# Every third output store of a tree-attention kernel gives its last sixteen rows to two small hardware DMAs

## The chip, the cores and the metric

The kernel runs on one core of one Trainium2 chip. The metric is the device time of one execution in microseconds (us), the median of three runs. A profile of one execution shows the engines of the core: TensorE (PE, with its weight loads as PEld), VectorE (DVE), ScalarE (ACT), GpSimd (POOL) and SyncE (SP), and beside them 16 DMA engines, which move data between HBM and SBUF for all of them. "Rows" below are SBUF partitions, of which there are 128.

## The reference

For 8 batches and 12 heads, 96 heads in all, each of 512 queries of 64 elements attends only to itself and its ancestors in a binary tree (the parent of node `i` is `(i - 1) // 2`):

```python
scores = np.einsum('bhqd,bhkd->bhqk', Q, K) * scale
scores = scores + (1 - mask) * (-1e9)
weights = np.exp(scores - np.max(scores, axis=-1, keepdims=True))
weights = weights / (np.sum(weights, axis=-1, keepdims=True) + 1e-10)
return np.einsum('bhqk,bhkd->bhqd', weights, V).astype(np.float32)
```

Q, K, V and the output are float32, 12.58 MB each.

## The kernel before, in words

Row `p` of a tile holds nodes `4p` to `4p + 3` of a head, so one head is 1 KB (256 float32) on each of the 128 rows, and that KB lies in one piece in HBM. Heads are worked on in pairs (48 of them, `NP`); two pairs make a quad of four heads (24, `NQ`), which is one output tile `of` and one store; two quads make a group of eight heads (12, `NO`), which is the unit of loading.

The main loop (line 498) makes one pass for each pair `i`: scores on TensorE (lines 310 to 351), their exponential on ScalarE (lines 323 and 347), the products with V for the pair before (`values`, line 366), the division by the sums on VectorE (`norm`, lines 392 and 395, which writes `of`), and the transposes of Q and K for a pair further on (line 275), which VectorE copies out of PSUM (line 301). V is spread into the order that the products need by copies on VectorE (lines 238 and 253), ScalarE (line 253) and GpSimd (line 224).

All loads but the first small ones, and 23 of the 24 stores, are DMAs that GpSimd issues[...]; the stores share that queue. `pool_program` (line 412) writes out their order by hand: for each group half of K, half of Q, all of V, the other half of K, then the four copies of line 224, the other half of Q, and then two stores, eight quads behind the loads' own count (`BEHIND`, line 409). Stores 0 to 13 go between the loads, stores 14 to 22 after them. A store is 512 KB: on each row four pieces of 1 KB. The output tiles have 15 buffers (line 158), so a quad can wait long for its store.

SyncE has almost nothing to do: it issues the first K load and two small loads of mask codes (8 rows and 40 rows, lines 175 and 176) at the start, and two of the three pieces of the last store at the end (lines 522 and 523; ScalarE issues the third). Between them its queue is idle.

Of the kernel before, what the change touches and what calls it, by code (L numbers as in the profile page):

```python
# [115 lines left out]
def kernel(  # L116
# [7 lines left out]
    nc = tc.nc  # L124
    B, H, S, D = Q.shape
    P = nc.NUM_PARTITIONS
# [3 lines left out]
    NP = 2 * NQ  # L130
# [9 lines left out]
    Or = out.rearrange("b h (p t) d -> p (b h) (t d)", t=4)  # L140
# [61 lines left out]
    qTs, kTs, kqps, obs, ets, ofs = {}, {}, {}, {}, {}, {}  # L202
# [10 lines left out]
    def load_k(o, h0=0, n=8):  # L213
        load(ksts, "kst", loads, Kr, o, h0, n)

    def load_q(o, h0=0, n=8):
        load(qsts, "qst", loads, Qr, o, h0, n)

    def load_v(o, h0=0, n=8):
        load(vsts, "vst", vloads, Vr, o, h0, n)  # L220

    def spread_top(eng, o, h0=0, h1=8):
        for j in range(4):
            eng.tensor_copy(  # L224
                out=vts[o % NV][32 * j:32 * j + 32, h0:h1, VTOP:VTOP + D],
                in_=vsts[o][0:32, h0:h1, UNITS[TOP + j][1], :],
            )
# [21 lines left out]
    def spread_l7(copy, o, quad, h0=0, h1=8):  # L249

        slot = 2 * (quad % 2)
        lower = quad < 2
        copy(  # L253
            out=tile_pair(o, 0, h0, h1, 1)[32 * quad:32 * quad + 32] if lower
            else tile_pair(o, 64, h0, h1, 0)[32 * quad - 64:32 * quad - 32],
            in_=swapped(vsts[o][32:64, h0:h1, slot + (not lower), :], D if lower else -D),
        )
# [21 lines left out]
    def transpose(i):  # L279
        kqp = psT.tile([P, 2, 1024], bf16, name="kqp")  # L280
        kqps[i] = kqp
        for t in range(4):
            for a in range(2):
                transpose_one(kqp[:, 0, :], i, a, t, _slot_layout(t)[1], ksts, perms[t])
        for t in range(4):
            for a in range(2):
                transpose_one(
                    kqp[:, 1, :], i, a, t, [_psum_unit(4 * QPOS[t] + j) for j in range(4)],
                    qsts, qperm,
                )  # L290
# [17 lines left out]
    def scores1(i):  # L308

        sp = psS.tile([P, 2, 512], fp32, name="s1")  # L310
        for a in range(2):
            nc.tensor.matmul(  # L312
                out=sp[:, a, :], lhsT=k1code[64 * a:64 * a + 64, :],
                rhs=q1code[64 * a:64 * a + 64, :], start=True, stop=False,
            )
        for a in range(2):
            nc.tensor.matmul(  # L317
                out=sp[:, a, :], lhsT=keys(i, a, TOP),
                rhs=qTs[i][64 * a:64 * a + 64, :, :].rearrange("p t c -> p (t c)"),
                start=False, stop=True,  # L320
            )
        et = etpool.tile([P, 2, 4, 128], bf16, name="e1")
        nc.scalar.activation(  # L323
            out=et[:, :, :, :].rearrange("p a t c -> p (a t c)"),
            in_=sp[:, :, :].rearrange("p a c -> p (a c)"),
            func=AF.Exp, scale=scale,
        )
        ets[i] = et

    def scores2(i):  # L330

        sp = psS.tile([P, 2, 4, 128], fp32, name="s2")
        for a in range(2):
            nc.tensor.matmul(  # L334
                out=sp[:, a, :, 32:128], lhsT=k2code[64 * a:64 * a + 64, :],
                rhs=q2code[64 * a:64 * a + 64, :].rearrange("p (t c) -> p t c", t=4),
                start=True, stop=False,
            )
        for tile2, lo, hi in ((2, 32, 192), (0, 192, 320), (1, 320, 384), (3, 416, 512)):
            for a in range(2):  # L340
                nc.tensor.matmul(  # L341
                    out=sp[:, a, :, :].rearrange("p t c -> p (t c)")[:, lo:hi],
                    lhsT=keys(i, a, TILE2[tile2]),
                    rhs=qTs[i][64 * a:64 * a + 64, :, :].rearrange("p t c -> p (t c)")[:, lo:hi],
                    start=False, stop=tile2 == 3, skip_group_check=tile2 in (2, 0),
                )
        nc.scalar.activation(  # L347
            out=e2s[i % NE][:, :, :, 32:128].rearrange("p a t c -> p (a t) c"),
            in_=sp[:, :, :, 32:128].rearrange("p a t c -> p (a t) c"),
            func=AF.Exp, scale=scale,  # L350
        )
# [31 lines left out]
    def norm(i):  # L383
        q, r = divmod(i, 2)
        if r == 0:
            ofs[q] = opool.tile([P, 4, 4, D], fp32, name="of")
        ob = obs[i][:, :, 0:261]
        part, bank = list(ob.ap[0]), list(ob.ap[1])
        sums = bass.AP(ob.tensor, ob.offset, [part, bank, [195, 2], [65, 2]])
        vals = obs[i][:, :, 1:261].rearrange("p a (t c) -> p a t c", c=D + 1)[:, :, :, 0:D]  # L390
        rec = small.tile([P, 2, 4, 1], fp32, name="rec")
        nc.vector.reciprocal(  # L392
            out=rec[:, :, :, :].rearrange("p a (x y) z -> p a x (y z)", x=2), in_=sums
        )
        nc.vector.tensor_tensor(  # L395
            out=ofs[q][:, 2 * r:2 * r + 2, :, :],
            in0=vals,
            in1=rec[:, :, :, :].to_broadcast([P, 2, 4, D]),
            op=ALU.mult,
        )  # L400

    def store(eng, q, h0=0, n=4):
        eng.dma_start(  # L403
            out=Or[:, 4 * q + h0:4 * q + h0 + n, :],
            in_=ofs[q][:, h0:h0 + n, :, :].rearrange("p h t d -> p h (t d)"),
        )


    BEHIND = 8
    NO = NQ // 2  # L410

    def pool_program():

        load_k(0, 2, 2)
        load_q(0, 2, 2)
        load_v(0, 0, 4)
        load_k(0, 4, 4)
        load_q(0, 4, 4)
        load_v(0, 4, 4)
        load_k(1, 0, 4)  # L420
        load_q(1, 0, 4)
        spread_top(nc.gpsimd, 0, 0, 4)
        load_v(1)
        load_k(1, 4, 4)
        load_q(1, 4, 4)
        spread_top(nc.gpsimd, 0, 4, 8)
        yield
        yield
        for o in range(2, NO):
            load_k(o, 0, 4)  # L430
            load_q(o, 0, 4)
            load_v(o)
            load_k(o, 4, 4)
            spread_top(nc.gpsimd, o - 1)
            load_q(o, 4, 4)
            yield
            for q in (2 * o - BEHIND, 2 * o + 1 - BEHIND):
                if q >= 0:
                    store(nc.gpsimd, q)
        for q in range(NQ - BEHIND, NQ - 1):  # L440
            yield
            store(nc.gpsimd, q)
            if q == NQ - BEHIND + 1:
                spread_top(nc.gpsimd, NO - 1)

    def spread_first(copy, quad, parts):

        for part in parts:
            if part < 4:
                spread_l7(copy, 0, part, 4 * quad, 4 * quad + 4)  # L450
            else:
                spread_leaves(0, part - 4, 4 * quad, 4 * quad + 4)

    def spread_vector(i):
# [4 lines left out]
        o, step = divmod(i + (2 if i > 4 else 1), 4)  # L459
        if 1 <= o < NO and step < 2:  # L460
            if i <= 4:
# [9 lines left out]
    def spread_scalar(i):  # L471

        if i == 1:
            spread_first(nc.scalar.copy, 1, (0, 1))
        o, quad = divmod(i + 1, 4)
        if 2 <= o < NO and quad < 2:
            spread_l7(nc.scalar.copy, o, quad)
        if i == 4:
            for quad in (0, 1):
                spread_l7(nc.scalar.copy, 1, quad)  # L480

    def pool_until(done, wanted):
        while done < wanted:
            next(program, None)
            done += 1
        return done
# [11 lines left out]
    for i in range(NP + 1):  # L498
        if i < NP:
            scores1(i)  # L500
            scores2(i)
            spread_scalar(i)
        if i == 1:
            transpose(2)
            evac(2)
            spread_first(nc.vector.tensor_copy, 1, (2, 3))
        if i >= 1:
            values(i - 1)
            norm(i - 1)
        for n in (1 if i == 0 else i + 2,):  # L510
            if n < NP:
                transpose(n)
                evac(n)
        if i == 0:
            spread_first(nc.vector.tensor_copy, 0, range(6))
        spread_vector(i)
        if steps < NO:
            steps = pool_until(steps, min((i + 11) // 4, NO))
        else:
            steps = pool_until(steps, min(steps + 2, NO + (i - 2) // 2 - (NQ - 1 - BEHIND)))  # L520
        if i == NP - 1:
            store(nc.sync, NQ - 1, 0, 2)
# [32 lines left out]
```

## Time and profile before

Three runs took 137.17, 137.59 and 138.16 us. The profiled execution has a span of 135.9 us from the first to the last instruction.

| engine | busy us | share of the span | instructions |
|---|---|---|---|
| TensorE | 109.6 | 81% | 2409 |
| VectorE | 105.0 | 77% | 220 |
| ScalarE | 106.8 | 79% | 123 |
| GpSimd | 96.0 | 71% | 140 |

Busy time is the sum of the instructions' durations; what counts more is what an engine waits for, and when. The profile also has a row for the DMA engines, with their mean busy share in 40 slices of the span, and a list of DMA queues: the GpSimd queue carries 30.68 MB, SyncE's queue 0.71 MB, ScalarE's 0.46 MB, and TensorE's instructions come in 19 transfers of 16 KB. A store that GpSimd issues takes 10.4 us (median) from issue to landing, the two pieces that SyncE issues at the end 5.4 and 4.7 us.

### The profile page before, as it was taken

The page shows a single profiled execution, that of the slowest core. Times are in us where ns is not written, and L with a number is a line of the kernel's source. Part 1 is how long each engine was busy: PE and PEld are TensorE (multiplying, and loading weights), DVE is VectorE, ACT ScalarE, POOL GpSimd, SP SyncE. Part 2 cuts the span into 40 slices and gives each one's busy share as a digit, 9 for nine tenths or more (in the row PEclk, how much of TensorE's full clock was granted, in tenths as well). Part 3 has the DMA queues.
Part 4 walks back from the last instruction along what each step waited for, and adds up shares of the span by engine and source line. Part 5 has one row for each costly group of instructions (what it writes and reads, how often), then busy time and mean ns, then how long its engine had stood idle before and what let it go on. Part 6 is the DMA issues. An engine that isn't in the chain of part 4 may idle for free.

```text
span 135.9 us, 5534 instructions
## 1 busy us (share of the span) xinstructions
PE 109.6 (81%) x2409; PEld 78.7 (58%) x2409; DVE 105.0 (77%) x220; ACT 106.8 (79%) x123; POOL 96.0 (71%) x140
## 2 busy tenths in 40 slices
PE   4977885996997989998979979879959679878700
PEld 1354664774775766766757657667737457647500
DVE  6559988798898897797897797997697697797510
ACT  4166789699699799897899799897897888897600
POOL 6987979398697984983974697597597597393200
PEclk9999999999999999999999999999999999999995
DMA  3999999999999999999999999999999999999980
GB/s 102 233 174 196 198 196 198 196 197 197 197 197 237 321 197 221 333 200 203 345 201 200 336 218 197 317 239 198 294 262 197 269 292 195 250 392 375 379 305 25
DMA packets 41978, 32.19 MB, mean 237 GB/s; under 512 B 1458, under 2 KB 39010, under 8 KB 41954
## 3 DMA queue, kind: packets, MB, share of 16 engines
q0 software_dynamic: 40640, 30.68, 124.7%
q1 hardware_dynamic: 754, 0.71, 1.6%
q10 hardware_dynamic: 560, 0.46, 1.0%
q8 instruction: 19, 0.31, 0.8%
q14 instruction: 5, 0.04, 0.1%
HBM read 37.87 MB, written 12.58 MB: 371 GB/s over the span
## 4 chain that ended last, share of the span: by engine, by line
DVE 37%; PE 36%; DMA 9%; ACT 7%; issue 5%; ACTq 0%; DVEq 0%
PE ob L366 14%; DVE of L395 11%; DVE vt L253 10%; DMA vst<-in_V_dram 9%; PE kqp L275 7%; DVE kq L301 7%; DVE vt L238 6%; PE s L312 5%; ACT e L323 4%; DVE rec L392 3%; PE s L317 3%; PE ob L263 3%; PE s L341 3%; ACT e L347 2%; PE s L334 2%
## 5 line engine op out<-in xcount | busy, mean ns | idle before, releaser
L323 ACT ACTIVATE e<-s 128x1024 bf16<-128x1024 f32 x48 | 49.0, 1020 | 16.2 <-PE s L317 15.7
L366 PE MATMUL ob<-vt,e 128*128 128x65 bf16 (+1 forms) x940 | 37.9, 197 | 10.5 <-DVE of L395 8.2
L366 PEld LDWEIGHTS <-e 128*128 128x128 bf16 (+1 forms) x960 | 30.6, 102 | 17.3 <-PE s L341 6.1
L224 POOL COPY vt<-vst 32x512 bf16<-32x512 bf16 (+1 forms) x52 | 31.5, 605 | 10.4 <-DMA vst<-in_V_dram 5.7
L347 ACT ACTIVATE e<-s 128x768 bf16<-128x768 f32 x48 | 38.4, 801 | 0.0
L301 DVE COPY kq<-kqp 128x1024 bf16<-128x1024 bf16 x48 | 32.7, 681 | 2.5 <-PE kqp L275 2.4
L395 DVE TENSOR_TENSOR of<-ob,rec 128x512 f32<-128x512 f32 x47 | 32.5, 691 | 1.6
L208 POOL DMA_DIRECT2D kst<-in_K_dram x24 | 18.5, 771 | 11.6 <-DMA vst<-in_V_dram 10.5
L253 ACT COPY vt<-vst 32x1024 bf16<-32x1024 bf16 (+1 forms) x24 | 24.1, 1002 | 1.7 <-DMA vst<-in_V_dram 1.0
L275 PE MATMUL kqp<-ptile,qst 128*64 128x128 bf16 x384 | 19.1, 220 | 2.5 <-DMA qst<-in_Q_dram 2.5
L275 PE MATMUL kqp<-ptile,kst 128*64 128x128 bf16 x384 | 19.5, 220 | 1.9 <-issue 1.8
L403 POOL DMA_DIRECT2D out_dram<-of x23 | 17.4, 762 | 3.7 <-DVE of L395 3.5
L208 POOL DMA_DIRECT2D qst<-in_Q_dram x24 | 18.4, 768 | 2.1 <-PE s L317 0.6
L392 DVE RECIPROCAL rec<-ob 128x8 f32<-128x8 f32 x47 | 9.7, 206 | 13.2 <-PE ob L366 12.6
L312 PE MATMUL s<-codes 64*128 64x512 bf16 x96 | 19.1, 386 | 0.8 <-issue 0.2
L341 PEld LDWEIGHTS <-kq 64*128 64x128 bf16 x384 | 15.8, 94 | 6.2 <-issue 0.7
L317 PE MATMUL s<-kq 64*128 64x512 bf16 x96 | 18.5, 376 | 0.7 <-DVE kq L301 0.7
L341 PE MATMUL s<-kq 64*128 64x128 bf16 (+3 forms) x384 | 17.7, 209 | 0.4 <-issue 0.4
L253 DVE COPY vt<-vst 32x1024 bf16<-32x1024 bf16 (+1 forms) x28 | 16.8, 600 | 0.6
L334 PE MATMUL s<-codes 64*128 64x384 bf16 x96 | 15.9, 323 | 0.4
L238 DVE COPY vt<-vst 64x1024 bf16<-64x1024 bf16 (+1 forms) x26 | 13.0, 499 | 3.7 <-DMA vst<-in_V_dram 1.9
L275 PEld LDWEIGHTS <-qst 128*64 128x64 bf16 x384 | 13.5, 110 | 3.3 <-DMA qst<-in_Q_dram 3.1
(24 smaller groups left out, 54.1 us busy)
## 6 DMA issues: line engine op xcount, KB each, us to landing
out_dram<-of POOLq DMA_DIRECT2D x23, 512.0 KB, 10.4
kst<-in_K_dram POOLq DMA_DIRECT2D x23, 256.0 KB, 11.6
qst<-in_Q_dram POOLq DMA_DIRECT2D x23, 256.0 KB, 9.6
vst<-in_V_dram POOLq DMA_DIRECT2D x11, 512.0 KB, 12.6
vst<-in_V_dram POOLq DMA_DIRECT2D x2, 256.0 KB, 6.1
first_k<-in_K_dram SPq DMA_DIRECT2D x1, 256.0 KB, 3.3
first_q<-in_Q_dram ACTq DMA_DIRECT2D x1, 256.0 KB, 3.6
out_dram<-of SPq DMA_DIRECT2D x1, 256.0 KB, 5.4
```

Of the source, the lines that this page charges most:

```text
L208: nc.gpsimd.dma_start(out=kept[o][:, h0:h0 + n, :, :].rearrange("p h t d -> p h (t d)"), in_=src[:, 8 * o + h0:8 * o + h0 + n, :],)
L224: eng.tensor_copy(out=vts[o % NV][32 * j:32 * j + 32, h0:h1, VTOP:VTOP + D], in_=vsts[o][0:32, h0:h1, UNITS[TOP + j][1], :],)
L253: copy(out=tile_pair(o, 0, h0, h1, 1)[32 * quad:32 * quad + 32] if lower else tile_pair(o, 64, h0, h1, 0)[32 * quad - 64:32 * quad - 32], ...
L275: nc.tensor.transpose(out=dst, in_=st[i // 4][:, 2 * (i % 4) + a, t, :], identity=perm)
L301: nc.vector.tensor_copy(out=kq[:, :, :, :].rearrange("p k (x y) c -> p k x (y c)", x=2), in_=src)
L312: nc.tensor.matmul(out=sp[:, a, :], lhsT=k1code[64 * a:64 * a + 64, :], rhs=q1code[64 * a:64 * a + 64, :], start=True, stop=False,)
L317: nc.tensor.matmul(out=sp[:, a, :], lhsT=keys(i, a, TOP), rhs=qTs[i][64 * a:64 * a + 64, :, :].rearrange("p t c -> p (t c)"), start=False, ...
L323: nc.scalar.activation(out=et[:, :, :, :].rearrange("p a t c -> p (a t c)"), in_=sp[:, :, :].rearrange("p a c -> p (a c)"), func=AF.Exp, s ...
L341: nc.tensor.matmul(out=sp[:, a, :, :].rearrange("p t c -> p (t c)")[:, lo:hi], lhsT=keys(i, a, TILE2[tile2]), rhs=qTs[i][64 * a:64 * a + 6 ...
L347: nc.scalar.activation(out=e2s[i % NE][:, :, :, 32:128].rearrange("p a t c -> p (a t) c"), in_=sp[:, :, :, 32:128].rearrange("p a t c -> p ...
L366: nc.tensor.matmul(out=ob[lo:hi, a, start_o:start_o + 65], lhsT=e[:, a, QPOS[t], lo:hi], rhs=vt[:, 2 * (i % 4) + a, col:col + 65], **flags,)
L395: nc.vector.tensor_tensor(out=ofs[q][:, 2 * r:2 * r + 2, :, :], in0=vals, in1=rec[:, :, :, :].to_broadcast([P, 2, 4, D]), op=ALU.mult,)
```

## The change

For the quads with `q % 3 == 1` (1, 4, 7, 10, 13, 16, 19 and 22, eight of them) GpSimd's store covers rows 0 to 111 only. Rows 112 to 119 and 120 to 127 go out in two DMAs of their own, of 32 KB each, which SyncE issues as soon as the quad's second `norm` is done. So these sixteen rows leave in time order of the computation, some eight quads before GpSimd's part of the same store. The work of the engines, the order of the loads and the output stay as they were. It is meant to shift a part of the output from GpSimd's queue to SyncE's idle one, and from all 16 DMA engines to those that an 8-row DMA runs on.

```diff
-    def store(eng, q, h0=0, n=4):
+    def store(eng, q, h0=0, n=4, rows=(0, 128)):
+        p = slice(*rows)
         eng.dma_start(
-            out=Or[:, 4 * q + h0:4 * q + h0 + n, :],
-            in_=ofs[q][:, h0:h0 + n, :, :].rearrange("p h t d -> p h (t d)"),
+            out=Or[p, 4 * q + h0:4 * q + h0 + n, :],
+            in_=ofs[q][p, h0:h0 + n, :, :].rearrange("p h t d -> p h (t d)"),
         )
+    def parted(q):
+        return q % 3 == 1
+    def store_main(q):
+        store(nc.gpsimd, q, rows=(0, PARTED if parted(q) else P))
+    def store_rest(q):
+        if parted(q):
+            for p in range(PARTED, P, 8):
+                store(nc.sync, q, rows=(p, p + 8))
     BEHIND = 8
+    PARTED = 112
...
-                    store(nc.gpsimd, q)
+                    store_main(q)
         for q in range(NQ - BEHIND, NQ - 1):
             yield
-            store(nc.gpsimd, q)
+            store_main(q)
...
             values(i - 1)
             norm(i - 1)
+            if i % 2 == 0 and i < NP:
+                store_rest(i // 2 - 1)
```

## The prediction

> **What bounds the kernel now.** I read the slices of the span first, then the stages, the queues, the waits near the end and the chain that ended last. In the slices the DMA row is full nearly throughout, and no other row is:
>
> ```profile
> DVE  6559988798898897797897797997697697797510
> ACT  4166789699699799897899799897897888897600
> DMA  3999999999999999999999999999999999999980
> ```
>
> In the table of stages (columns: stage, its us, busy us of PE, PEld, DVE, ACT, POOL with counts, clock, DMA share, GB/s) the DMA engines are over 1, since packets of one engine overlap, until 130 us:
>
> ```profile
> 98.00:117.60 19.60, 16.20 (x388) 12.11 (x389) 15.38 (x29) 16.66 (x20) 13.87 (x20) 1.00 1.36 244
> 117.60:126.00 8.40, 6.71 (x140) 4.64 (x139) 7.21 (x15) 7.25 (x9) 5.72 (x8) 1.00 1.07 370
> 126.00:130.00 4.00, 2.31 (x52) 1.65 (x49) 2.23 (x5) 1.92 (x3) 0.76 (x1) 1.00 1.00 374
> 130.00:135.90 5.90, 0.00 (x0) 0.00 (x0) 0.00 (x0) 0.00 (x0) 0.00 (x0) 0.66 0.37 131
> ```
>
> The last 5.9 us hold nothing but stores. The packets in the trace say what one row costs: GpSimd's loads come as 512 B packets that start 41.2 ns apart on one engine, its stores as one 4 KB packet a row, one each 164 ns. An engine has 36352 / 16 = 2272 load packets and 2944 / 16 = 184 store packets: 93.6 + 30.2 = 124 us of a span of 136. So DMA is the bound, with the computation close behind. The waits from 100 us on show where the two meet (engine, line, releaser: us, times, longest), and the chain has one V load in it:
>
> ```profile
> DVE vt L238 <- DMA vst<-in_V_dram: 1.9, 2, 1.0
> PE kqp L275 <- DMA qst<-in_Q_dram: 0.6, 1, 0.6
> ```
>
> ```profile
> 104.92 12.62 DMA vst<-in_V_dram
> ...
> 128.99 0.69 DVE of L395
> ```
>
> VectorE stops 1.0 us each for the last two V loads and TensorE 0.6 for the last Q load; after V at 117.5 us come 12 us of computation, then the last stores.
>
> **The 16 engines are not level.** A transfer is complete when its slowest engine is, and the trace has the 16 moments at which each completion counter rises. For the last V load they lie, after the first, at 0, 0.12, 0.13, 0.39, 0.98, 1.24, 1.42, 1.77, and 2.10, 2.27, 2.33, 2.35, 2.58, 2.63, 2.98, 3.18 us: the load waits 3.2 us for its last engine. The queues name the cause:
>
> ```profile
> q0 software_dynamic: 40640, 30.68, 124.7%
> q8 instruction: 19, 0.31, 0.8%
> ```
>
> 0.8% of 16 x 135.9 us over 19 transfers is 0.92 us for each 16 KB of instructions, during which one engine moves nothing else. After eight of them (67 us) eight engines are some 1.07 us further back than at 15 us, after sixteen (117 us) the same eight about 2.1; the other eight gained none. So the instruction transfers go round eight of the sixteen, and these eight are the late ones. At the end the pattern is the same: at 125.5 us the late eight stand at 2.12 to 4.58, the early eight at 0 to 1.79.
>
> [...]the 8-row load of mask codes raised its counter in 8 steps after one early one, the 40-row load in 10.[...]
>
> **The change part by part.** Per parted store:
> - removed: on every engine one row of GpSimd's store, 0.164 us;
> - added: on engines 0 to 7 two rows of four 1 KB packets. The hardware stores and first loads of this kernel show 46 ns a packet, starting 42 apart: 2 x 4 x 46 = 0.37 us, 0.33 at the least.[...] I take 0.37[...].
> - so engines 8 to 15 have 0.164 us less, engines 0 to 7 0.20 us more. Eight times: -1.31 and +1.64 us.
> - issue: SyncE needs 0.39 us a DMA (lines 522 and 523). Its queue waits for the second `norm` of the quad, but all that it has behind that is the next such pair and, after the last, the final store:
>
> ```profile
> SPq L403 <- DVE of L395: 127.3, 2, 126.5
> ```
>
>  So the wait delays no one. GpSimd's DMA instructions (0.76 us) stay as many; 15 output buffers hold. I cost these at nothing.
>
> **Which half is the late one** decides the sign. No view names the engines. The trace gives a clue: the 40-row load[...]. Six of its ten ends lie at 4.21 to 4.39 us, and three, at 4.307, 4.334 and 4.363, are each followed on their engine by 16 packets and an end of GpSimd's first load (4.970, 4.997, 5.027). Followed on through ends at 6.987, 7.014, 7.043 to 8.327, 8.351, 8.381, they are third to fifth of the five leading engines, none of which ever takes an instruction transfer.[...] Stalls at 6.5 to 7.5 us make the middle step unsure. I take it: the change unloads the late half.
>
> At the end the late half's last engine then goes from 4.58 to about 4.58 - 7 x 0.164 = 3.43 at 125.5 us, the early half's from 1.79 to 1.79 + 7 x 0.20 = 3.2: still behind, but little. The end comes up to 1.3 us earlier. Against that, by the last V load SyncE has sent seven pairs (2.6 us on engines 0 to 7) while only five shortened stores (-0.8) have passed: early half 1.77 + 1.76 = 3.5, late half 3.18 - 0.82 = 2.4. V lands 0.3 us later, and with it the computation; the last stores, which today trail `norm` (129.7) by 4.9 us behind backlog, absorb that. The sum: -1.3 + 0.3 = -1.0, 136.6 us.
>
> **Rivals.**
> - The late half is 0 to 7. Then V and Q land 1.7 us later, the stalls in the waits grow, and the end has +1.6: 139.2, slower. For it: nothing but the weak step above. 15%.
> - Hidden: the 0.3 us at V, or a second engine of the early half that becomes last, eats the gain: 137.5. For it: both halves come within 0.3 us of each other. 27%.
> - [...]engines 0 to 7 carry 8 us more, of which some 3 were slack: 142. 6%.
> - Waits for V and Q (2.5 us together) shrink too, and all of it reaches the end: 135.6. For it: at the V load before, 3.18 falls to about 2.8. 12%.
> - The forecast, 136.6: 40%.
>
> **How the numbers follow.** Faster by over 1% is below 136.2: the case of 135.6 and the lower third of the forecast's spread (0.5 us either way), 0.12 + 0.2 with a little of the rest, 0.35. Slower than 139.0: [...], 0.17. Between: 0.48. The range[...]: 135.7 to 139.2.
>
> **What would show it.** Right: 16 DMAs of 32 KB on SyncE's queue landing in a few us; at 117 us completion spread over both halves, with the last V load within 0.5 us of 117.5; the stores-only stretch at the end about 1 us shorter. Wrong: packets of SyncE's queue well over 46 ns[...]; V and Q landing over 1 us later with longer stalls on lines 238 and 275 (wrong half); or an unchanged tail.

## The result, and the profile after

The changed kernel takes 141.28 us (median of four runs, 140.83 to 141.62), the kernel before 137.78 us beside it (137.17 to 138.16). The ratio is 1.0256, with a 95% interval of 1.0206 to 1.0307: 3.5 us slower. Measured again later (e17 below), the same change came to 1.0211 (1.0150 to 1.0273); that run gives a second profile of it. The forecast was 136.6 us with a range up to 139.2, so both the side and the size were missed. Executions over 1.5% above the fastest of their kernel are left out of every ratio here as slow (one of e3 took 318.6 us), which also lowers the ratio of a kernel that scatters widely of itself: with every execution counted, e9 below has 1.0108 instead of 1.0082, and e6 1.0158 instead of 1.0114.

The span grew from 135.9 to 139.1 us. The slices of the changed kernel, VectorE, ScalarE and DMA, and below them the bytes that the DMA engines moved:

```profile
DVE  6459989698878897768797697997897697697500
ACT  4156789599679799888899698998896897897500
DMA  3999999999999999999999999999999999989970
GB/s 96 228 172 193 195 196 198 203 197 196 199 199 255 289 199 244 316 198 221 323 203 222 316 203 223 322 212 216 309 220 209 310 219 204 335 332 309 309 247 24
```

The DMA row is as full as before and no other row filled up. In the stages (same columns as the table of before, cut at the same work: up to the last V load, to some 3.7 us ahead of the end of the last `norm`, to that end, and the rest):

```profile
100.50:120.10 19.60, 16.15 (x382) 11.91 (x379) 14.98 (x28) 16.75 (x19) 13.37 (x19) 1.00 1.37 239
120.10:128.50 8.40, 6.26 (x138) 4.43 (x134) 7.23 (x15) 6.98 (x9) 5.69 (x8) 1.00 0.96 330
128.50:132.15 3.65, 2.29 (x52) 1.65 (x49) 2.20 (x5) 1.90 (x3) 0.72 (x1) 1.00 0.94 310
132.15:139.10 6.95, 0.00 (x0) 0.00 (x0) 0.00 (x1) 0.00 (x0) 0.00 (x0) 0.56 0.42 134
```

After the last V load the DMA engines are nearly as busy as before (0.96 and 0.94 against 1.07 and 1.00), but they move 330 and 310 GB/s where they moved 370 and 374. Each byte became dearer, and nearly all of that is after the last V load: up to it the rate is 239 GB/s against 244. The stretch after the last `norm`, forecast to be 1 us shorter, is 6.9 us instead of 6.2. The other part lies ahead of it. First the issues of the V loads, before and after (the number after "to" is the moment of the last issue), then two lines of the changed kernel's chain:

```profile
L208 POOL DMA_DIRECT2D vst<-in_V_dram x13: 777/884/927, 2.8 to 104.9; - x13
```

```profile
L208 POOL DMA_DIRECT2D vst<-in_V_dram x13: 760/884/929, 2.8 to 107.1; - x13
```

```profile
96.43 12.80 DMA vst<-in_V_dram
...
131.46 0.69 DVE of L395
```

The last `norm` ends at 132.15 us and not at 129.68, since the last V load was complete at 120.02 us and not at 117.54. That load took hardly longer (12.9 us against 12.6); it was issued 2.2 us later. The V load before it, the first line of the chain here, was already complete 2.2 us later than before (109.22 us against 107.02), so most of the delay had gathered over the groups before. In this profile 2.5 of the 3.2 us come from there and 0.7 from the end. In the second profile the shares are 1.8 and 1.9 us, with the same sum within 0.5: where the time shows is not fixed, so the experiments below look at the total.

The parts that the prediction took for granted are there. The queues of the changed kernel, its DMA issues, and what SyncE's queue waits for:

```profile
q0 software_dynamic: 40512, 30.15, 121.8%
q1 hardware_dynamic: 1394, 1.23, 2.9%
q8 instruction: 19, 0.31, 0.8%
```

```profile
out_dram<-of POOLq DMA_DIRECT2D x8, 448.0 KB, 10.5
out_dram<-of SPq DMA_DIRECT2D x16, 32.0 KB
```

```profile
SPq L404 <- DVE of L395: 121.8, 8, 20.2
```

Eight stores of 448 KB, sixteen DMAs of 32 KB, half a megabyte moved from GpSimd's queue (30.68 MB before) to SyncE's, and eight waits of SyncE for `norm` with nothing but its own pieces behind them. Before the last of them, the last packet of a pair moved 4.3 to 5.2 us after the pair's first issue, where GpSimd's stores need 10.5 us to land, so SyncE's packets did not wait behind GpSimd's. Each small DMA raises its completion counter in 8 steps after one early one, and GpSimd's stores of 112 rows raise theirs in 16, as those of 128 do: they run on eight engines and on sixteen. "Engines 0 to 7", in the prediction and below, stands for the eight that carry an 8-row DMA; which ones they are is not shown.

The packets tell the two rates apart (worked out from the packet records: GpSimd's store packets of 4 KB, one row each, and the small ones of 1 KB):

```
kernel    4 KB packets between loads    after 124 us: number, mean ns, over 230 ns    1 KB packets between loads
before    162 to 163 ns                 608, 174.2, 10                                -
after     162 to 163 ns                 685, 202.2, 115                               384, 55.6 ns
```

In the changed kernel a figure takes GpSimd's stores of 112 and of 128 rows together. Between the loads the shorter stores leave the mean where it was (162.8 ns against 162.5). At the end, where nothing but stores is left, they don't.

### The profile page after: what moved, and what is told of

Same layout as the page of the kernel before. It is cut to its first block, busy times and chain, and to the rows that moved or that the text cites. A ratio compares the mean times of both kernels' runs of the same rounds, so it can differ in the third digit from the quotient of the medians.

```text
span 139.1 us, 5562 instructions
## 1 busy us (share of the span) xinstructions
PE 109.9 (79%) x2409; PEld 79.3 (57%) x2409; DVE 105.4 (76%) x220; ACT 107.1 (77%) x123; POOL 95.5 (69%) x140
## 4 chain that ended last, share of the span: by engine, by line
PE 29%; DVE 28%; DMA 26%; issue 7%; ACT 3%; POOL 1%; DVEq 0%; ACTq 0%; POOLq 0%
PE ob L366 11%; DMA vst<-in_V_dram 9%; DMA kst<-in_K_dram 9%; DMA qst<-in_Q_dram 8%; DVE vt L253 8%; DVE of L395 8%; PE kqp L275 6%; DVE kq L301 5%; DVE vt L238 5%; PE s L312 3%; PE ob L263 3%; PE s L317 2%; DVE rec L392 2%; PE s L341 2%; ACT e L347 2%
## 5 line engine op out<-in xcount | busy, mean ns | idle before, releaser
L238 DVE COPY vt<-vst 64x1024 bf16<-64x1024 bf16 (+1 forms) x26 | 13.5, 521 | 3.5 <-DMA vst<-in_V_dram 1.6
L275 PEld LDWEIGHTS <-kst 128*64 128x64 bf16 x384 | 12.9, 111 | 4.9 <-issue 3.7
## 6 DMA issues: line engine op xcount, KB each, us to landing
out_dram<-of POOLq DMA_DIRECT2D x15, 512.0 KB, 10.5
out_dram<-of POOLq DMA_DIRECT2D x8, 448.0 KB, 10.5
```

Of the source, the lines that this page charges most:

```text
L275: nc.tensor.transpose(out=dst, in_=st[i // 4][:, 2 * (i % 4) + a, t, :], identity=perm)
```

## The experiments

Each is set against the kernel before on the same chip. "Parted" quads are those whose store is divided. Quads 1, 4, 7, 10 and 13 are stored by GpSimd between the loads (early), 16, 19 and 22 after the last V load (late). Times in us are the ratio less 1, times 137.7. A moment read from a single profile is sure to about 1 us only: three kernels that do the same work up to the last V load (before, and the two below with only late stores altered and no small DMAs) had it at 117.54, 117.69 and 118.55 us.

| kernel | late store of GpSimd | small DMAs | ratio (95%) | us | after 124 us: ns a packet | last `norm` to end, us |
|---|---|---|---|---|---|---|
| before | 128 rows | none | 1 | 0 | 174 | 6.2 |
| the change | 112 | early, late | 1.0256 (1.0206 to 1.0307) | +3.5 | 202 | 6.9 |
| early quads only (e1) | 128 | early | 1.0032 (1.0012 to 1.0053) | +0.4 | 176 | 6.5 |
| late quads only (e2) | 112 | late | 1.0225 (1.0173 to 1.0277) | +3.1 | 200 | 8.5 |
| late shape alone (e9) | 112 | none | 1.0082 (1.0057 to 1.0106) | +1.1 | 201 | 5.8 |
| late small ones alone (e11) | 128 | late, extra | 1.0044 (1.0019 to 1.0070) | +0.6 | 173 | 5.7 |
| early small ones alone (e12) | 128 | early, extra | 1.0095 (1.0061 to 1.0130) | +1.3 | 171 | 5.1 |
| late in two of 64 rows (e6) | 64 and 64 | none | 1.0114 (1.0077 to 1.0150) | +1.6 | 201 | 8.3 |
| late by whole head (e5) | 128 | one of 128 KB each | 1.0051 (1.0027 to 1.0075) | +0.7 | 176 | 5.4 |

### Early against late

One theory was that the late stores lose the time through their shape; the rival, that the five early pairs push back the V loads.

```diff
-        return q % 3 == 1
+        return q % 3 == 1 and q < 14      # e1: early quads only
+        return q % 3 == 1 and q >= 14     # e2: late quads only
```

> Only the five parted stores that leave between the loads (quads 1, 4, 7, 10, 13); the three in the store-only stretch at the end are whole again. Theory HALF (the small DMAs load engines 0 to 7, one of which is the last to complete V; a pair costs them 8 x 53 ns less 164 ns, net 0.26 us): the last V load lands 5 x 0.26 = 1.3 us later than before, time about 139.1. Theory TAIL (stores of 112 rows slow each other where all engines store): the 4 KB packets from 124 us on fall back to about 175 ns, and the time is close to before, 137.8 to 138.3. Theory EARLY (the sixteen rows overtake loads, whatever engines they run on): like HALF, 5/7 of it.

> Only the parted stores of quads 16, 19 and 22; the five between the loads are whole. HALF: by the last V load two pairs have gone and no store is shorter, so engines 0 to 7 are 2 x 0.42 = 0.85 us later; the last V load about 0.8 us later, time 138.5 or less. TAIL: the 4 KB packets of the store-only stretch take over 200 ns as in the changed kernel, and most of its loss is here: 139.5 to 141.

The early five cost 0.4 us, the late three 3.1, both in the range of theory TAIL, and the two make up the whole (3.5). Five eighths of the change explain an eighth of the loss.

### Parts of the change, all eight quads

```diff
-            if i % 2 == 0 and i < NP:
-                store_rest(i // 2 - 1)         # e3: no small DMAs
...
-            for p in range(PARTED, P, 8):
-                store(nc.sync, q, rows=(p, p + 8))
+            store(nc.sync, q, rows=(PARTED, P))   # e4: one of 16 rows
```

e3 leaves rows 112 to 127 of the eight quads unwritten.

> All eight stores of 112 rows stay and the small DMAs are left out, so rows 112 to 127 of eight quads are not written. HALF and EARLY: every engine has 5 x 0.164 = 0.8 us less before the last V load and 1.3 us less in all, so 136.3 to 137. TAIL: the packets of the store-only stretch stay at over 200 ns although no small DMA runs, and the time stays above before's, 138 to 139.5.

> The sixteen rows leave in one DMA of 16 rows[...], at the same moments on the same queue. HALF: no engine gets more than 4 x 53 - 164 = 0.05 us a quad, the last V load at 117.5 to 118.2, so the loss but for the tail's goes: 138 to 139. EARLY: as slow as the changed kernel, 141. TAIL: the 4 KB packets of the store-only stretch stay over 200 ns.

e3: 1.0064 (1.0030 to 1.0098), 0.9 us slower than before, though every engine has 8 x 0.164 = 1.3 us less to move. Its packets after 124 us take 194 ns. So shorter stores lose time with nothing added. e4: 1.0157 (1.0112 to 1.0203), above the 138 to 139 us of theory HALF. Sixteen rows in one DMA instead of two, meant for sixteen engines instead of eight, win back 1.4 us (0.4 to 2.3, by the two intervals); 2.2 us stay, with packets of 206 ns at the end. The engines are then complete 2.9 us apart at the last V load, those of the change 5.3. So the imbalance that the prediction turned on is, by these figures, less than half of the loss.

### The shape of a late store

Three ways to alter only GpSimd's stores of quads 16, 19 and 22. e5 parts by heads: GpSimd stores three heads and SyncE the fourth, both on 128 rows. e6 has GpSimd store rows 0 to 63 and 64 to 127 in two DMAs. e9 stores 112 rows and leaves rows 112 to 127 of these three quads unwritten.

```diff
+        return q % 3 == 1 and q >= 14
...
-        store(nc.gpsimd, q, rows=(0, PARTED if parted(q) else P))
+        store(nc.gpsimd, q, n=3 if parted(q) else 4)                     # e5, and store(nc.sync, q, 3, 1)
+        for rows in ((0, 64), (64, 128)) if parted(q) else ((0, 128),):  # e6, no small DMAs
+            store(nc.gpsimd, q, rows=rows)
```

> In quads 16, 19 and 22 SyncE takes the fourth head of the quad on all 128 rows (128 KB, one DMA on 16 engines) instead of sixteen rows; GpSimd stores three heads on 128 rows. As many bytes leave early as in the run with parted stores after the last V load, and twice over. TAIL (the shape of 112 rows is what hurts): a GpSimd packet is 3 KB here and takes 125 to 140 ns, none over 200 ns as a rule; 137.0 to 138.2. If it is the early sending or a second queue beside GpSimd's that slows the tail: 139.5 to 141, as with 112 rows.

> In quads 16, 19 and 22 GpSimd stores rows 0 to 63 and rows 64 to 127 in two DMAs; SyncE sends nothing early. Four rows go to each engine in place of eight or seven. If the odd seven rows are the cause, nothing slows: 137.8 and packets of 175 ns. [...]the packets of the tail take over 200 ns as with 112 rows, and the time is 139 or more.

> In quads 16, 19 and 22 GpSimd's store covers rows 0 to 111 and nothing else is changed: no small DMA at all, and rows 112 to 127 of these quads are not written. Beside the run with parted stores after the last V load (1.0225 of before) this leaves out the six small DMAs and keeps the shape. If the shape of 112 rows is what slows the tail: packets over 200 ns on average after 124 us and still slower than before, 1.005 to 1.02, though 192 KB less is written. If the small DMAs in flight together with the tail are needed for it: 0.993 to 1.0.

The stages at the end (columns as above) of the kernel before, of e9 and of e5:

```profile
124.00:128.00 4.00, 3.55 (x72) 2.48 (x68) 2.27 (x6) 3.45 (x4) 0.76 (x1) 1.00 1.03 384
128.00:132.00 4.00, 0.67 (x16) 0.50 (x16) 1.38 (x3) 0.00 (x0) 0.00 (x0) 0.99 0.94 340
```

```profile
124.00:128.00 4.00, 3.81 (x86) 2.71 (x83) 2.47 (x6) 3.02 (x4) 0.79 (x2) 1.00 1.01 322
128.00:132.00 4.00, 1.42 (x37) 1.03 (x33) 1.80 (x4) 0.99 (x2) 0.46 (x1) 1.00 0.96 320
```

```profile
124.00:128.00 4.00, 3.81 (x84) 2.77 (x84) 2.84 (x6) 3.03 (x5) 0.91 (x2) 1.00 1.01 372
128.00:132.00 4.00, 1.79 (x48) 1.34 (x42) 1.80 (x4) 1.37 (x2) 0.74 (x1) 0.99 0.97 354
```

e9 has less to move than the kernel before and no DMA more, and it is 1.1 us slower: 322 GB/s at a DMA share of 1.01. e6 writes every row with two DMAs of half the rows, on average four rows to an engine (64 / 16), and loses 1.6 us with packets of 201 ns, so an odd seven rows isn't the cause. e5 sends a part early on SyncE's queue just as the change does, but on all rows, and keeps 372 GB/s with packets of 176 ns (GpSimd's packets stayed at 4 KB there; its expectation had 3 KB); its stretch after the last `norm` is 5.4 us, so where its 0.7 us come from is open, but a slow end isn't seen. In e9 97 of 619 packets take over 230 ns, which makes (201.4 - 174.2) x 619 / 16 = 1.05 us more for each engine; the three rows that each engine no longer stores take 3 x 0.174 = 0.5 us off. In the profiled execution of e9 the span is 0.6 us above before's and the end no longer, so the packets show that the stores became slower, and for the size the ratio counts.

### Stores alone

To measure a row by itself, one execution with groups of eight GpSimd stores of constant data and nothing else (all computation and all loads are left out), with different rows, to the output's place and to a scratch tensor in which each row's 4 KB lie in one piece.

```diff
+    group(((0, 128),), "out")
+    group(((0, 112),), "out")
+    group(((0, 64),), "out")
+    group(((64, 128),), "out")
+    group(((0, 96),), "out")
+    group(((0, 128),), "scratch")
+    group(((0, 112),), "scratch")
+    group(((0, 64),), "scratch")
```

> Not the reference's computation: it writes a constant. Groups of eight stores that GpSimd issues back to back, nothing else beside them, the next group only when the last has landed: on 128 rows, 112, 64 (0 to 63), 64 (64 to 127), 96 into the output; then 128, 112 and 64 rows into a scratch tensor in which a row's 4 KB lie in one piece. If the shape slows stores by itself: 128 rows 164 to 175 ns a packet, 112, 96 and 64 rows over 200 in every group, on the output and on the scratch tensor alike if it is the SBUF side, on the output alone if it is the HBM side. If it needs engines that are out of step with each other, as after the loads: all groups at 160 to 180 ns.

The stages of that kernel, one in the middle of each group in the order above (the last two columns are again DMA share and GB/s):

```profile
4.00:16.00 12.00, 0.00 (x0) 4.39 (x6) 1.00 0.99 325
21.00:33.00 12.00, 0.00 (x0) 3.63 (x6) 1.00 0.95 285
37.00:47.00 10.00, 0.00 (x0) 3.35 (x6) 1.00 0.95 192
52.00:61.00 9.00, 0.00 (x0) 2.75 (x5) 1.00 0.96 207
65.00:77.00 12.00, 0.00 (x0) 3.60 (x6) 1.00 0.87 248
81.00:91.00 10.00, 0.00 (x0) 2.88 (x6) 1.00 1.01 390
95.00:108.00 13.00, 0.00 (x0) 2.78 (x6) 1.00 0.84 275
112.00:122.00 10.00, 0.00 (x0) 2.80 (x6) 1.00 0.94 202
```

On all rows the engines move 325 to 390 GB/s, on 112 rows 275 to 285, on 96 rows 248, on 64 rows 192 to 207. The engines of the 64-row groups are occupied and not idle (share 0.94 to 0.96), and a packet takes 300 to 319 ns in the mean against 168 to 197 on all rows. The 112-row groups have a median of 159 ns, but a quarter and a fifth of their packets take over 230: most rows go at full speed and some do not. Their mean, 218 and 199 ns, is above that of 128 rows at either destination, and the engines are idle for a part besides (share 0.95 and 0.84). The rates to the two destinations differ, most for 128 rows (325 and 390 GB/s), but fewer rows lose at both, so the layout in HBM alone isn't the cause; the number of rows is. Why fewer rows make packets longer is not shown.

### The small DMAs alone

All stores stay whole, and the small DMAs come on top, into a scratch tensor, so rows 112 to 127 of the quads concerned are written twice. e7 has all eight pairs (one 4 KB packet a row), e11 the late three and e12 the early five (four 1 KB packets a row, as in the change).

```diff
+    def extra(q):
+        if q % 3 == 1:                     # e11: and q >= 14; e12: and q < 14
+            for p in range(112, P, 8):
+                nc.sync.dma_start(
+                    out=scratch[...],
+                    in_=ofs[q][p:p + 8, :, :, :].rearrange("p h t d -> p h (t d)"),
+                )
```

> All GpSimd stores keep 128 rows as in the kernel before; the sixteen small DMAs of 8 rows are added, into a scratch tensor in HBM that nothing reads. HALF: engines 0 to 7 get 0.42 us a quad with nothing taken off, 2.9 us by the last V load; if the latest engine is among them the last V load comes up to 2.9 us later and the time is 140 to 141.5; if it is not, at most 1.5 us later and 138 to 139.3. TAIL: the 4 KB packets of the tail stay at about 175 ns.

> GpSimd stores every quad on all 128 rows as before; the six small DMAs of quads 16, 19 and 22 are added, 1 KB pieces, into a scratch tensor of HBM laid out like the output, so nothing of the output is moved and the rows 112 to 127 of these quads are written twice. Engines 0 to 7 get 3 x 0.42 = 1.3 us more. With the change these six DMAs came on top of the 112-row stores and cost 2.0 us there (140.69 with both, 139.21 with the shape alone, 1.0225 against 1.0082). Theory additive: the same 2.0 us here, about 139.8. Theory that they cost what their engine time is, and no more: up to 1.3 us, 138.6 to 139.1. Theory that only together with the slow stores do they cost: under 0.5 us, 137.8 to 138.3. Stores after 124 us about 175 ns a packet in all three.

> The same for quads 1, 4, 7, 10 and 13: ten small DMAs of 1 KB pieces added into a scratch tensor, all stores whole. Engines 0 to 7 get 5 x 0.42 = 2.1 us more, all of it before the last V load. Theory that the late engines among 0 to 7 pass this on: last V load at about 119.6, as with the eight added pairs of 4 KB packets (119.63), time +1.4 to +2.1, 139.2 to 139.9. Theory that most of it is taken up, as the change's own five early pairs suggest (1.0032, with 0.82 us of rows removed): +0.4 to +0.9, 138.2 to 138.7.

e7: 1.0105 (1.0041 to 1.0169), +1.4 us; its packets take 173 ns, so a pair gives engines 0 to 7 0.35 us each, and not the 0.42 of its expectation. Its time is in the range for a latest engine outside 0 to 7, its V load is not. It puts the last V load at 119.63 us, past the 117.5 to 118.6 of the three kernels above, and then has only 5.1 us from the last `norm` to the end. e12: +1.3 us (0.8 to 1.8), between the ranges of its two theories and nearer to the first. Beside the change's own early pairs (e1, +0.4) that is 0.9 us more (0.3 to 1.4), and what these have less is five rows of 0.164 us, 0.82. So between the loads a removed row gives back about what it was priced at, and the small packets cost time, 0.26 us a pair of the 0.42 that they occupy an engine. e11: +0.6 us, between its second and third theory, less than the 1.3 us of engine time, and well under the 2.0 us by which e2 exceeds e9. The two parts of the late quads come to 1.1 + 0.6 = 1.7 us one at a time and to 3.1 (2.4 to 3.8) together.

### What makes the late parts cost more together

In the trace the second small DMA of quad 22 takes 1.55 us to issue, against 0.30 for the earlier ones, and the final store's pieces stand behind it on SyncE's queue, with issues of 1.12 and 1.53 us (0.40 and 0.39 before). Was it that queue? e13 leaves quad 22 whole, e14 parts it alone, and e15 keeps the whole change and sends the final store from ScalarE; e16 is e15 again, e17 the change again, and e18 the kernel before with the same move.

```diff
-        return q % 3 == 1
+        return q % 3 == 1 and q < 22           # e13
+        return q == 22                         # e14
...
-            store(nc.sync, NQ - 1, 0, 2)
-    store(nc.sync, NQ - 1, 2, 1)
+            store(nc.scalar, NQ - 1, 0, 2)     # e15, e16; e18 from the kernel before
+    store(nc.scalar, NQ - 1, 2, 1)
```

> As the change, with seven parted quads: 22 is stored whole, so no pair of small DMAs stands ahead of the final store on SyncE's queue. With the change that pair is issued at 128.93 us, its second DMA takes 1.55 us to issue (0.30 for the earlier pairs), and the final store's pieces behind it take 1.12 and 1.53 us to issue (0.40 and 0.39 before). Theory that the queue behind the last pair makes the end late: 1.0 to 1.5 us below the change, 139.6 to 140.2, and the final pieces issued in about 0.4 us. Theory that the 112-row stores and the share of engines 0 to 7 do it, and the long issues only show full engines: an eighth of the loss goes, 0.2 to 0.5 us, 140.7 to 141.1, with issues still of about 1 us.

> Quad 22 alone is parted: one 112-row store, the last that GpSimd issues, and one pair of small DMAs ahead of the final store. Theory of the queue behind the last pair: +1.0 to +1.5 us, 138.8 to 139.4. Theory of stores and engine shares: a third of what quads 16, 19 and 22 cost together at most, and 0.1 us from the pair: 0 to +0.7 us, 137.8 to 138.5.

> The whole change, eight parted quads, but all three pieces of the final store go out from ScalarE's queue, after its last exponential; nothing stands behind the pair of quad 22. Theory of the queue behind the last pair: 1.0 to 1.5 us below the change, 139.8 to 140.3. Theory of stores and engine shares: as the change, or 0.3 to 0.4 us later since three issues follow each other on one queue: 141.0 to 141.7.

> The whole change with the final store's three pieces on ScalarE's queue, as in the run before (139.50 to 141.79 us in four runs, too wide to judge), now beside the change itself on the same chip. Theory of the queue behind the last pair of SyncE: 1.0 to 1.5 us below the change. Theory of stores and engine shares: level with the change, within 0.4 us.

> The change itself, unaltered, for the comparison on the same chip: 141.3 us as measured first (1.0256), with either theory.

> The kernel before with only the final store's pieces moved to ScalarE's queue: what that move costs by itself. The first piece goes out about 2 us later than on SyncE's queue but still before the last norm, and the two after the norm are issued one after the other, 0.38 us apart: 0 to +0.4 us, 137.6 to 138.0. If it comes to more, that is to be taken off from what the move does to the change.

e13: 1.0163 (1.0086 to 1.0239), +2.2 us; that is in the range of the queue theory, but the interval reaches the other's. e14: 1.0079 (1.0041 to 1.0116), +1.1 us for quad 22 alone, about a third of what the late three cost, between the two ranges. e15 decided nothing: its four executions spread from 139.5 to 141.8 us (ratio 1.0171, 1.0128 to 1.0214). e16 decides: 1.0271 (1.0230 to 1.0312) beside 1.0211 (1.0150 to 1.0273) for the change itself (e17) and 0.9990 (0.9964 to 1.0017) for the move alone (e18). With nothing behind the last pair the change is as slow. The issues of the output in e16's trace after 115 us (least, median and most ns):

```profile
L404 ACTq DMA_DIRECT2D out_dram<-of x3: 390/1191/1410, 130.4 to 133.1; - x3
L404 SPq DMA_DIRECT2D out_dram<-of x2: 278/858/1438, 128.4 to 128.7; - x2
```

On ScalarE's queue, where no small DMA is, the pieces take as long to issue, and e12, which has no late pair, and e18, which has no small DMA at all, show 1.12 and 1.18 us for their last piece. So the theory of SyncE's queue falls. Nor do the long issues themselves account for the end: GpSimd's own last store is complete at 133.4 us before, 136.4 in the change and 138.4 in e16, and the final pieces follow it by 1.2, 1.5 and 0.9 us. What is late is GpSimd's store.

What makes shape and small DMAs together cost 1.4 us more than apart (give or take 0.9, by the three intervals) stays open. e4 shows that it isn't the share of engines 0 to 7 alone: with the sixteen rows in one DMA and the engines within 2.9 us of each other at the last V load, its stretch from the last `norm` to the end is still 8.6 us. The counters of GpSimd's last store give a hint. Before, its last engine is complete 1.0 us after the last but one; in e2, in e16, in the second profile of the change and in e6 it is 2.7, 3.4, 2.1 and 2.2 us, so there a single engine holds up the end, in e6 without any small DMA. In the first profile of the change and in e9 it is 0.3 us or less. Which engine it is, and why, is not shown.

### Which engines are late

The kernel before with marks: after quads 2, 4, 6 and so on, two DMAs into a scratch tensor that read rows 112 to 112 + n - 1, n from 8 down to 1, so that the engines which carry them fall back by two packets.

```diff
+    MARKS = {2: 8, 4: 8, 6: 4, 8: 4, 10: 2, 12: 2, 14: 1, 16: 1}
+    def extra(q):
+        if q in MARKS:
+            n = MARKS[q]
+            for r in range(2):
+                nc.sync.dma_start(
+                    out=scratch[q, r, 0:n, :, :],
+                    in_=ofs[q][112:112 + n, :, :, :].rearrange("p h t d -> p h (t d)"),
+                )
```

> A look, not a time: small DMAs into a scratch tensor at known moments mark engines in the completion times of the loads: after quads 2 and 4 two DMAs of 8 rows (engines 0 to 7 fall back 0.4 us), after 6 and 8 of 4 rows[...], after 10 and 12 of 2 rows[...], after 14 and 16 of 1 row[...]. If the eight engines that take instruction transfers are 8 to 15, as the prediction took it, none of them falls back at the first two marks; if they are 0 to 7, all of them; if both halves have some, part of them.

Two packets of 171 ns are 0.34 us. The offsets of the 16 engines at the load completed just before the second mark (40.8 us) and at the one just after it, in us from the first engine, and those that must have moved for the two rows to match (the choice that fits best):

```
before the mark  0 .125 .218 .254 .266 .332 .447 .488 .534 .592 .645 1.118 1.129 1.209 1.319 1.765
after the mark   0 .235 .274 .284 .345 .505 .557 .803 .851 .943 1.002 1.143 1.259 1.465 1.675 2.120
moved by 0.34    .125 .447 .488 .592 .645 1.118 1.319 1.765
not moved        0 .218 .254 .266 .332 .534 1.129 1.209
```

Moving eight engines fits to 12 ns (root mean square), any other number to 35 at best, so eight carry an 8-row DMA, as assumed. One other choice of eight fits nearly as well (13 ns); it has 1.129 moved in place of 1.118. By either, of the five engines that are over 1.1 us back three carry the DMA, among them the last one, and two don't. So the late engines lie in both halves. Four instruction transfers had run by then; that the five are late through these is likely for four of them at most, and not shown. The marks of 4, 2 and 1 rows could not be read apart, so single engines stay unnamed.

## Why the prediction was wrong, point by point

- **DMA is the bound.** Held: a DMA row full to the end, and the time follows what the DMA engines are given and how fast they move it.
- **Small packets, 46 ns each, 0.37 us a pair.** Near: at 41.2 to 42.4 us, 25.8 to 27.0 and 71.8 to 73.2 us the engine time that the other packets leave over is 53 to 55 ns for each small one, 0.42 us a pair. Eight pairs: +2.1 us net on engines 0 to 7 instead of +1.64.
- **"On every engine one row of GpSimd's store, 0.164 us" removed.** This is the step that failed. It holds between the loads (e12 against e1: 0.9 us for five rows). At the end it doesn't, because the rows that remain are no longer 0.164 us each: once three stores have 112 rows, GpSimd's packets there take 201 ns in the mean instead of 174. Forecast for the late three was -0.5 us; measured for the shape alone was +1.1 (0.8 to 1.5). The step priced what was taken away at the row's price and left the rest of the store at its old one, with no bound from the other side.
- **The takers are one half, so the change unloads the late half.** Failed, as its weak step was said to allow; it rested on numbers of engines that no trace here shows. The late engines lie in both halves and the last one is among those that carry an 8-row DMA (e8). At the last V load the engines of the change are complete 5.3 us apart (5.5 in the second profile), where they were 3.2 us apart before, are 2.9 in e4 with the rows in one DMA, and were forecast at 3.5. The rival with the late half at 0 to 7 (139.2 us) had V late, as it came. So the early five cost +0.4 us where five removed rows were to give -0.8. That is the smaller error: 1.2 us, against 3.6 us for the late three (-0.5 forecast, +3.1 measured), of which 1.6 us is the shape (1.1 and the 0.5 not gained), 0.6 the small packets beside whole stores, and 1.4 comes only with both. (The two make 4.8 us where the whole miss is 4.5, since the forecast had 0.3 us for a later V.)
- **V a little later, absorbed by the stores that trail.** The mechanism held where stores are whole: e7 and e12 have V 1.5 to 2.1 us later and a stretch after the last `norm` of 5.1 us instead of 6.2. With small DMAs and 112-row stores both at the end nothing is absorbed: 6.9 and 8.1 us in the two profiles of the change, 8.5 in e2. The last V load at 120.0 us, over 1 us late, was one half of the sign named for a wrong half; the other half, longer stalls, hardly came (line 238 stops for 1.1 and 1.2 us at the last two V loads, and stopped for 1.0 us at each before).
- **Issue and SyncE's wait cost nothing.** Held as far as is known, though the text overlooked that issues can lengthen to 1.5 us at the end; with the final pieces on another queue (e16) the change is no faster.
- **The rival of 142 us** came nearest to the number, but placed the loss at the small DMAs, with 8 us more on engines 0 to 7. Between the loads these took 0.42 us a pair, 3.4 us for eight; GpSimd's stores at the end were slowed (202 ns a packet against 174). So it was near by luck, and why those stores slow is not shown. It had 6% because the cost was looked for on the wrong operation.

## What to carry to other kernels

When a DMA is made shorter by rows, price the whole DMA that remains and not only the rows taken off: while loads were mixed in, the shape made the mean packet no longer (162.8 ns against 162.5), and where stores ran back to back it made the mean packet 16% longer (174 to 202 ns). If a part of a store has to leave early, divide it along the free dimension and keep all 128 rows (1.0051 against 1.0225 here). Before work is moved to particular DMA engines, find out with marks which ones are late; none of the versions tried that write the whole output, the change included, beat the kernel before.

## What the hardware showed that was not expected

- Stores of 64 rows alone move 192 to 207 GB/s against 325 to 390 on 128 rows, with the engines occupied (e10). Two of them that together cover all rows are no substitute for one of 128: three such late stores cost 1.6 us (e6).
- With 112-row stores among them, GpSimd's stores take 162 to 163 ns a row between loads and 202 in the mean at the end, where one packet in six takes over 230.
- Hardware DMA packets of 1 KB occupy an engine 53 to 55 ns when mixed with loads; at the start of the kernel 42 apart.
- Issuing a small DMA takes 0.28 to 0.43 us in the middle of the kernel. At the end the second one of quad 22 takes 1.4 to 1.7 us, and a piece of the final store up to 1.4 us on ScalarE's queue (e16) and 2.7 on SyncE's (e17). Moving the pieces between the queues changed nothing that the runs could tell.
